# Four block-sum steps instead of three in most gate-and-up pairs of a two-layer encoder, with the matching order of steps and of the work around them

## The chip, the cores and the metric

The kernel runs on one core of one Trainium2 chip. The metric is the device time of one execution in microseconds. The engines go by these names: PE is TensorE (matmuls; PEld its weight loads), DVE is VectorE, ACT is ScalarE, POOL is GpSimd, SP is the engine that issues most loads.

## The reference

Two layers on 256 tokens of 2048 features, all in float32. Layer 0 mixes tokens by attention, layer 1 by a gated recurrence; each layer then has a feed-forward part with 5632 hidden features. Per layer:

```
x = x + mixer(rms_norm(x, g_mix))
x = x + (silu(h @ w_gate) * (h @ w_up)) @ w_down      # h = rms_norm(x, g_ffn)
```

The feed-forward parts hold most of the matmuls. The change touches these and the place where layer 0 hands over to layer 1.

## The kernel before

**Three matmuls for one product.** Every float32 operand is split into a rounded part `hi` (fp32r) and the rest `lo`. A product is hi*hi + hi*lo + lo*hi, three matmuls (`product`, L354 to L359). The tokens are the stationary side (128 x 128 tiles, two token halves), the weights the moving side, 512 columns wide.

**Splitting the weights.** `load_half` (L126) loads a half tile of 128 x 1024 weights over SP's queue into one of five `raw` buffers; ACT rounds it into `hi` (L141), DVE subtracts to get `lo` (L142). Both have five buffers as well.

**Pairs.** `project_pair` (L345) computes two groups of 512 output columns at once. For gate and up these are the same columns of `w_gate` and `w_up`. There are 11 such pairs ("units") in a layer, each with eight steps over the 2048 inputs, a step being two input tiles of 128. The hidden features are worked in three parts of 12, 16 and 16 tiles (`PARTS`): three units, then four, then four. After each part, two down pairs multiply its hidden tiles into the 2048 outputs, with six steps in part 0 and eight in parts 1 and 2. The last down pair of layer 0 is worked one column group at a time.

**Block-sum steps.** A plain step is a 2 x 2 block product (two token halves by two column groups, over two input tiles): eight products, 24 matmuls. Some steps are worked with seven products, 21 matmuls (Strassen's scheme in Winograd's form). These need sums and differences of the weight blocks (`seven_forms`, L308) and of the input blocks (`x_forms`, L333). One of the two weight half tiles is combined by a pair of POOL transfers, a plain one and an accumulating one, into `sr` (two buffers, `fetch_next`, L299). SP loads a quarter into `wx`. DVE adds three blocks (L319, L323, L324), ACT rounds (L321, L322, L326), and DVE splits (L325, L327, L328). `wx`, `wxh` and `wxl` have one buffer each. Four of the seven products of a pair collect in four PSUM banks of their own (`p1`, `q5`, `q6`, `q7` from `ps_m`). After the last block-sum step of a pair, `merge` (L399) combines them into `fg` and `fu`, with one ACT copy and four DVE operations.

**Which steps.** `THREE` gives the block-sum steps of a pair as input step numbers 1, 3 and 5. The first unit of a layer has two (3 and 5), the others three. Down pairs with eight steps have three, part 0's have none, and the last down pair of layer 0 has none. `pair_plan` (L154) works the steps up to the last block-sum step for both column groups together, and the rest one group at a time.

**The end of a unit.** `done` (L839) adds the PSUM sums to the merged ones (L843, L846) and applies SiLU and the gating (L847). Then the hidden tile is turned by a 32 x 32 transposition (L860) into `tb`, by sixteen ACT copies (L866) into `tf`, and by a split (L873, L874). These pieces are put on the list `owed` and emitted during the next pair's steps by `settle`.

**What sets the order.** PE's instructions run in program order. The other engines' order comes from a scheduler, with explicit ties on top: `in_line` keeps the weight splits of ACT and of DVE in order, `follow` ties one instruction behind another, and `not_after` together with `settled` puts an instruction ahead of the DVE split that comes some halves later. `later` puts off a piece by a number of half-steps (`clock`).

**The hand-over between layers.** `Norm.add` prepares the next normalised input from each finished 512 columns: squares (L491), transposition (L496), copies into `tf` (L503), and scaled and split operands (L478, L479). For the last columns `finish` (L518) works out the inverse root mean square first, and `spread` brings it into a row by a small matmul (L536), 20 half-steps later (`NORM`). Then `project_two` and `conv_branch` begin the recurrence.

Of the kernel before, what the change touches and what calls it, by code (L numbers as in the profile page):

```python
# [27 lines left out]
PARTS = [12, 16, 16]  # L28
THREE, TWO, SHORT = (1, 3, 5), (2, 5), 6
READY = 6  # L30
FIRST_STEPS = (0, 1, 2, 4, 3, 6, 5, 7)
# [10 lines left out]
WARM = 10  # L42
NORM = 20
FIRST = 6
# [26 lines left out]
def trunk(ctx, tc, w, out):  # L71
# [45 lines left out]

    def not_after(i, ahead=3):
        due.setdefault(taken[0] + ahead, []).append(i)

    def settled(i, n):
        for k in [k for k in due if k <= n]:
            for j in due.pop(k):
                follow(i, j)

    def load_half(src, n, pieces=1, then=None, before=None):  # L126
        raw = wp.tile([P, HALF, P], F32, tag="raw", name=nm("raw"), bufs=5)
        hi = wp.tile([P, HALF, P], F32R, tag="hi", name=nm("hi"), bufs=5)
        lo = wp.tile([P, HALF, P], F32R, tag="lo", name=nm("lo"), bufs=5)
        for i in range(pieces):  # L130
            sl = slice(i * n // pieces, (i + 1) * n // pieces)
            newest["load"] = sync.dma_start(out=raw[:, sl, :], in_=src[:, sl, :])
        newest["raw"] = raw
        if then:
            then()
        if before:
            before(raw)
        for i in range(pieces):
            sl = slice(i * n // pieces, (i + 1) * n // pieces)
            newest["tiles"] = hi, lo  # L140
            newest["cast"] = in_line("act", act.copy(hi[:, sl, :], raw[:, sl, :]))  # L141
            rest = in_line("dve", dve.tensor_tensor(lo[:, sl, :], raw[:, sl, :], hi[:, sl, :].bitcast(F32), ALU.subtract))  # L142
            settled(rest, taken[0] - 1)
        return [(hi[:, i, :], lo[:, i, :]) for i in range(n)]
# [12 lines left out]
    def unit_seven(i):  # L157
        return THREE[1:] if i == 0 else THREE

    def unit_plan(i):  # L160
        steps = range(KT // 2) if i else FIRST_STEPS
        return pair_plan(steps, 1 + steps.index(unit_seven(i)[-1]))
# [8 lines left out]
    def down_seven(n, alone):  # L171
        return () if alone else () if n == SHORT else THREE

# [171 lines left out]
    def project_pair(xs, forms, plan, middle, done, ready=None):  # L345
# [19 lines left out]
        for i, (n, cols) in enumerate(plan):  # L365
            if n in forms:
                s1, s2, s3, s4 = forms[n]
                b11, b21, t3, b22, t1, t2, t4 = seven_forms()
                settle(3)
                if n == seven[0]:  # L370
                    p1, q6, q5, q7 = (ps_m.tile([P, WIDE], F32, tag="pm", name=nm("pm")) for _ in range(4))
                last = n == seven[-1]
                product(p1, tokens(2 * n, 0), b11, last)
                product(bank(0, 0), tokens(2 * n + 1, 0), b21)
                product(bank(1, 0), s4, b22)
                product(q7, s3, t3, last)
                product(q5, s1, t1, last)
                product(q6, s2, t2, last)
                product(bank(0, 1), tokens(2 * n + 1, 1), t4)
                if last:  # L380
                    middle(p1, q5, q6, q7)
                continue
            if len(cols) == 1 and i and len(plan[i - 1][1]) == 2:
                settle(-1)
                if ready:
                    ready()
            end = n == plan[-1][0]
            for j in cols:
                half()
                if i:  # L390
                    settle(2 if len(owed) > 6 else 1)
                hi, lo = (flat(t) for t in newest["tiles"])
                for a in range(2):
                    for k in range(2):
                        product(bank(j, a), tokens(2 * n + k, a), (hi[:, k, :], lo[:, k, :]), end and k == 1)
                if end:
                    done(j, banks[j])

    def merge(p1, q5, q6, q7):  # L399
# [4 lines left out]
        dve.tensor_tensor(g[:, 1, :], q7, g[:, 1, :], ALU.subtract)  # L404
        dve.tensor_tensor(u[:, 1, :], u[:, 0, :], q7, ALU.subtract)
        return g, u
# [58 lines left out]
    class Norm:  # L465
# [6 lines left out]
        def operand(self, x, wide=False):  # L472
# [5 lines left out]
            i = act.activation(hi, x, AF.Copy, scale=g)  # L478
            dve.scalar_tensor_tensor(lo, x, g, hi.bitcast(F32), ALU.mult, ALU.subtract)  # L479
            self.xs.append(t)  # L480
# [3 lines left out]
        def add(self, c):  # L484
# [4 lines left out]
            def first():  # L489
                for a in range(2):  # L490
                    act.activation(tmp("nj", (P, WIDE), mybir.dt.bfloat16, 1), x_tok[:, a, c, :], AF.Square, accum_out=self.sums[:, a, c : c + 1])  # L491
                fields["behind"] = self.finish() if last else [line.get(e) for e in ("act", "dve")]
                fields["b"] = fp[0].tile([P, 2, FOUR, P], F32, tag="tb", name=nm("tb"))
                fields["f"] = fp[0].tile([P, 8, FOUR, 32], F32, tag="tf", name=nm("tf"))
                for a in range(2):
                    dve.transpose(fields["b"][:, a, :, :], x_tok[:, a, c, :])  # L496

            def copies(q):
                b, f = fields["b"], fields["f"]
                behind = fields["behind"] if last else [line.get(e) for e in ("act", "dve")]  # L500
                for i in range(4):
# [5 lines left out]
            def operands():  # L507
                for k in range(FOUR):
                    self.operand(fields["f"][:, :, k, :], True)
                for n in THREE[1:] if self.seven else ():  # L510
                    if FOUR * c <= 2 * n < FOUR * c + FOUR:
# [6 lines left out]
        def finish(self):  # L518
# [4 lines left out]
            if not self.seven:  # L523
                return prev[0], self.spread()


        def spread(self):
            dg = tmp("ndg", bufs=1)
            for a in range(2):
                i = dve.tensor_scalar(dg[:, a * P : (a + 1) * P], ident, self.rt[:, a : a + 1], None, ALU.mult)  # L530

# [7 lines left out]

            later(NORM, stage)  # L540
            return i

# [288 lines left out]
    def ffn(norm, nxt):  # L831
# [4 lines left out]
        def unit(hid, hid_units, forms, parts, i):  # L836
# [21 lines left out]
            def transposes():  # L858
                kept["b"], kept["f"] = (fp[0].tile([P, 2 * FOUR, P], F32, tag=n, name=nm(n), bufs=1) for n in ("tb", "tf"))
                dve.transpose(kept["b"], got[1])  # L860

            def copies(q):
                b = kept["b"][:].rearrange("p (a i) (k t) -> p a i k t", a=2, k=FOUR)
                f = kept["f"][:].rearrange("p q (k t) -> p q k t", k=FOUR)
                for i in range(4):
# [3 lines left out]
            def split_tiles():  # L869
                f = kept["f"][:].rearrange("p q (k t) -> p k q t", k=FOUR)  # L870
                h = act_tiles()
# [7 lines left out]

            owed.extend([transposes, *(partial(copies, q) for q in range(4)), split_tiles])  # L880

        line.update(act=None, dve=None)
# [118 lines left out]
    for b in range(-1, NBLK):  # L1001
# [9 lines left out]
        if nxt:  # L1011
            accs = (project_sum(nr.xs) for _ in range(2)) if blk else project_two(nr.xs, FOUR)
            nxt.xcs = [conv_branch(2 * b + 2 + i, t) for i, t in enumerate(accs)]
# [108 lines left out]
```

## Time and profile before

| | us |
|---|---|
| median of three runs | 1966.99 (1964.8 to 1967.59) |
| the profiled execution | 1964.75 |
| its span, first to last instruction | 1963.0 |
| layer 0's feed-forward part | 259.7 to 949.9 |
| layer 1's feed-forward part | 1271.2 to 1963.0 |
| granted TensorE clock | 1.00 throughout |

The stages' bounds are read from where the matmuls of each part begin. Rows of the profile give start and length in us, the engine, the line of the kernel, and what is written from what; rows that group instructions give their count, their busy time, the mean length in ns, and the idle time of the engine before them with what ended it. A window of stretches gives each engine's busy time in each.

### The profile page before, as it was taken

How to read it: one execution, taken by the hardware profiler on the slowest of the kernel's cores; microseconds unless marked ns; L12 is line 12 of the kernel's file. 1: busy time of each engine (PE TensorE's matmuls, PEld its weight loads, DVE VectorE, ACT ScalarE, POOL GpSimd, SP SyncE). 2: the span in 40 equal slices, each digit the busy share in tenths (PEclk: the TensorE clock that was granted, in tenths of full speed). 3: DMA queues.
4: the chain of work that ended last, by engine and by line, in shares of the span. 5: the costliest groups of instructions: out<-in, count | busy, mean ns of one | idle time of the engine just before them, and what ended most of it. 6: DMA issues, size and time to landing. Idle time of an engine off the chain costs nothing.

```text
span 1963.0 us, 27585 instructions
## 1 busy us (share of the span) xinstructions
PE 1954.5 (100%) x9665; PEld 1660.3 (85%) x9665; DVE 1686.6 (86%) x2274; ACT 1344.2 (68%) x2051; POOL 222.3 (11%) x317
## 2 busy tenths in 40 slices
PE   9999999999999999999999999999999999999999
PEld 8888888888888888888899998888888888888887
DVE  6776989858999989999788986998768999989997
ACT  6666767655677556777799996767646776567763
POOL 0011000000011100101034331001001010011010
PEclk9999999999999999999999999999999999999999
DMA  8543667756677876776555546567757777677784
GB/s 340 186 140 140 209 207 243 237 202 225 207 247 243 267 247 215 232 233 232 193 176 174 195 160 219 194 205 239 250 189 226 239 239 256 232 242 236 233 261 164
DMA packets 134059, 430.75 MB, mean 219 GB/s; under 512 B 15008, under 2 KB 15904, under 8 KB 133664
## 3 DMA queue, kind: packets, MB, share of 16 engines
q1 hardware_dynamic: 109296, 362.11, 52.9%
q0 software_dynamic: 24480, 66.86, 13.2%
q8 instruction: 76, 1.25, 0.2%
q14 instruction: 63, 0.52, 0.1%
q10 hardware_dynamic: 144, 0.02, 0.0%
HBM read 426.83 MB, written 2.10 MB: 219 GB/s over the span
## 4 chain that ended last, share of the span: by engine, by line
PE 98%; ACT 1%; DVE 1%; issue 0%; DMA 0%; DVEq 0%; ACTq 0%
PE acc L356 63%; PE pm L356 12%; PE acc L272 10%; PE acc L410 3%; PE acc L409 3%; PE acc L411 3%; PE pm L272 1%; PE pm L410 1%; PE pm L409 1%; PE pm L411 1%; PE pm L743 1%; PE pm L775 1%; PE pm L761 0%; ACT sg L607 0%; ACT L607 0%
## 5 line engine op out<-in xcount | busy, mean ns | idle before, releaser
L142 DVE TENSOR_TENSOR lo<-raw,hi 128x1024 fp32r<-128x1024 f32 (+1 forms) x621 | 748.4, 1229 | 130.6 <-ACT hi L141 127.7
L141 ACT CAST hi<-raw 128x1024 fp32r<-128x1024 f32 (+1 forms) x621 | 638.0, 1046 | 310.4 <-PE acc L356 163.3
L356 PE MATMUL acc<-hi,xg 128*128 128x512 f32 x1920 | 612.7, 389 | 0.0
L356 PE MATMUL acc<-hi,act 128*128 128x512 f32 x1370 | 433.7, 390 | 0.2 <-DVE gl L920 0.2
L356 PEld LDWEIGHTS acc<-hi,xg 128*128 128x128 f32 x1920 | 360.4, 188 | 74.8
L356 PE MATMUL acc<-lo,xg 128*128 128x512 f32 x960 | 373.4, 389 | 0.0
L356 PEld LDWEIGHTS acc<-hi,act 128*128 128x128 f32 x1370 | 257.2, 188 | 53.6 <-DVE gl L920 0.7
L356 PE MATMUL acc<-lo,act 128*128 128x512 f32 x685 | 266.6, 389 | 0.0
L356 PEld LDWEIGHTS acc<-lo,xg 128*128 128x128 f32 x960 | 180.2, 188 | 37.4
L326 ACT CAST wxh<-raw 128x1024 fp32r<-128x1024 f32 x85 | 89.3, 1051 | 91.3 <-DVE raw L324 91.3
L356 PEld LDWEIGHTS acc<-lo,act 128*128 128x128 f32 x685 | 128.6, 188 | 26.0
L866 ACT COPY tf<-tb 32x256 f32<-32x256 f32 x352 | 142.1, 404 | 10.9 <-DVE tb L860 7.0
L409 PE MATMUL acc<-xg,hi 128*128 128x256 f32 x512 | 144.9, 283 | 1.1 <-ACT xg L478 1.1
L410 PE MATMUL acc<-xg,hi 128*128 128x256 f32 x512 | 144.8, 283 | 0.1
L411 PE MATMUL acc<-xg,lo 128*128 128x256 f32 x512 | 144.4, 282 | 0.0
L304 POOL DMA_DIRECT2D sr<-in_w_up_dram x64 | 35.6, 557 | 763.5 <-DVE lo L325 598.1
L321 ACT CAST hi<-sr 128x1024 fp32r<-128x1024 f32 x85 | 89.3, 1051 | 37.6 <-PE acc L356 27.1
L322 ACT CAST wxh<-wx 128x512 fp32r<-128x512 f32 x85 | 52.8, 621 | 90.1 <-DVE wx L319 55.0
L328 DVE TENSOR_TENSOR wxl<-raw,wxh 128x1024 fp32r<-128x1024 f32 x85 | 103.3, 1215 | 7.7 <-ACT wxh L326 7.5
L272 PE MATMUL acc<-hi,xg 128*128 128x512 f32 x320 | 107.6, 396 | 0.5 <-ACT hi L141 0.5
L325 DVE TENSOR_TENSOR lo<-sr,hi 128x1024 fp32r<-128x1024 f32 x85 | 103.6, 1218 | 0.0
L409 PEld LDWEIGHTS acc<-xg,hi 128*128 128x128 f32 x512 | 97.9, 191 | 1.3 <-ACT xg L478 1.3
(212 smaller groups left out, 3174.5 us busy)
## 6 DMA issues: line engine op xcount, KB each, us to landing
raw<-in_w_gate_dram SPq DMA_DIRECT2D x176, 512.0 KB, 5.3
raw<-in_w_down_dram SPq DMA_DIRECT2D x155, 512.0 KB, 5.1
raw<-in_w_up_dram SPq DMA_DIRECT2D x112, 512.0 KB, 5.4
sr<-in_w_up_dram POOLq DMA_DIRECT2D x64, 512.0 KB, 4.9
raw<-in_w_in_dram SPq DMA_DIRECT2D x64, 512.0 KB, 4.4
raw<-in_w_qkv_dram SPq DMA_DIRECT2D x46, 512.0 KB, 4.4
raw<-in_w_o_dram SPq DMA_DIRECT2D x32, 512.0 KB, 3.5
wx<-in_w_up_dram SPq DMA_DIRECT2D x64, 256.0 KB, 4.6
```

Of the source, the lines that this page charges most:

```text
L141: newest["cast"] = in_line("act", act.copy(hi[:, sl, :], raw[:, sl, :]))
L142: rest = in_line("dve", dve.tensor_tensor(lo[:, sl, :], raw[:, sl, :], hi[:, sl, :].bitcast(F32), ALU.subtract))
L272: pe.matmul(accs[a], x, wt[:, k, :], start=(k0 + k == 0 and n == 0), stop=(end and k == 1 and n == 2))
L321: in_line("act", act.copy(hi, raw))
L325: settled(in_line("dve", dve.tensor_tensor(lo, raw, hi[:].bitcast(F32), ALU.subtract)), taken[0] - 1)
L326: in_line("act", act.copy(xh[:, 1:, :], r1))
L328: in_line("dve", dve.tensor_tensor(xl[:, 1:, :], r1, xh[:, 1:, :].bitcast(F32), ALU.subtract))
L356: pe.matmul(acc, a, b, start=id(acc) not in begun, stop=last and i == 2)
L409: pe.matmul(o, hi, x[:, :S], start=start, stop=False)
L410: pe.matmul(o, hi, x[:, S:], start=False, stop=False)
L411: pe.matmul(o, lo, x[:, :S], start=False, stop=stop)
L866: n = act.copy(f[32 * i : 32 * i + 32, q::4, :, :], b[32 * q : 32 * q + 32, :, i, :, :])
```

## The change

- `MORE = (3, 5, 1, 6)`: the third and later units of each layer have four block-sum steps. `LATER_STEPS` orders their eight input steps so that these stand at places 1, 3, 5 and 7. The first two units stay as they are. Part 0's down pairs, which had none, get the steps 1 and 3.
- The block differences of the inputs of step 6, needed for that, are made once a layer, after the second unit. Room for them comes from `tf`, which is dropped: turned tiles use the merged tile `fg` again.
- In a pair's first step, if it is a block-sum step, nothing owed is emitted, and the products of `bank(0, 1)` and `bank(1, 0)` come last.
- `merge`'s last operation gets a bound by `not_after`, and the bounds now exist for ACT as well as for DVE.
- At the hand-over the root mean square comes behind the last operands (which get bounds on both engines), and its small matmul 31 half-steps later instead of 20. The last copies are no longer tied behind it. The two column groups that begin the recurrence are both projected before either goes on.

```diff
+MORE = (3, 5, 1, 6)
+LATER_STEPS = (3, 0, 5, 2, 1, 4, 6, 7)
-NORM = 20
+NORM = 31
...
-    def not_after(i, ahead=3):
-        due.setdefault(taken[0] + ahead, []).append(i)
-    def settled(i, n):
-        for k in [k for k in due if k <= n]:
+    def not_after(i, ahead=3, eng="dve"):
+        due.setdefault((taken[0] + ahead, eng), []).append(i)
+    def settled(i, n, eng="dve"):
+        for k in [k for k in due if k[0] <= n and k[1] == eng]:
...
+            settled(newest["cast"], taken[0] - 1, "act")
...
-        return THREE[1:] if i == 0 else THREE
+        return THREE[1:] if i == 0 else THREE if i == 1 else MORE
-        steps = range(KT // 2) if i else FIRST_STEPS
+        steps = FIRST_STEPS if i == 0 else tuple(range(KT // 2)) if i == 1 else LATER_STEPS
...
-        return () if alone else () if n == SHORT else THREE
+        return () if alone else THREE[:2] if n == SHORT else THREE
...
-                settle(3)
+                if i:
+                    settle(3)
...
-                product(bank(0, 0), tokens(2 * n + 1, 0), b21)
-                product(bank(1, 0), s4, b22)
+                first = [(bank(0, 0), tokens(2 * n + 1, 0), b21)]
+                rest = [(bank(0, 1), tokens(2 * n + 1, 1), t4), (bank(1, 0), s4, b22)] if n == plan[0][0] else []
+                for t in first if rest else first + [(bank(1, 0), s4, b22)]:
+                    product(*t)
...
-                product(bank(0, 1), tokens(2 * n + 1, 1), t4)
+                for t in rest or [(bank(0, 1), tokens(2 * n + 1, 1), t4)]:
+                    product(*t)
...
-        dve.tensor_tensor(u[:, 1, :], u[:, 0, :], q7, ALU.subtract)
+        not_after(dve.tensor_tensor(u[:, 1, :], u[:, 0, :], q7, ALU.subtract))
...
-                fields["behind"] = self.finish() if last else [line.get(e) for e in ("act", "dve")]
+                if last and self.seven:
+                    self.finish()
-                fields["f"] = fp[0].tile([P, 8, FOUR, 32], F32, tag="tf", name=nm("tf"))
+                fields["f"] = fp[1].tile([P, 8, FOUR, 32], F32, tag="fg", name=nm("fg"), bufs=1)
...
+                if last and not self.seven:
+                    for e, i in zip(("act", "dve"), newest["operand"]):
+                        not_after(i, 4, e)
+                    self.finish()
...
-                kept["b"], kept["f"] = (fp[0].tile([P, 2 * FOUR, P], F32, tag=n, name=nm(n), bufs=1) for n in ("tb", "tf"))
+                kept["b"] = fp[0].tile([P, 2 * FOUR, P], F32, tag="tb", name=nm("tb"), bufs=1)
+                kept["f"] = got[0][:].rearrange("p a (q t) -> p (a q) t", t=P)
...
+            if i == 1:
+                n = MORE[-1]
+                norm.forms[n] = x_forms(norm.xs[2 * n], norm.xs[2 * n + 1], f"nf{n}")
...
-            accs = (project_sum(nr.xs) for _ in range(2)) if blk else project_two(nr.xs, FOUR)
+            accs = (project_sum(nr.xs) for _ in range(2)) if blk else list(project_two(nr.xs, FOUR))
```

More of the change, by code (lines that the diff above doesn't have):

```diff
@@ L478, in operand @@
             i = act.activation(hi, x, AF.Copy, scale=g)
-            dve.scalar_tensor_tensor(lo, x, g, hi.bitcast(F32), ALU.mult, ALU.subtract)
+            newest["operand"] = i, dve.scalar_tensor_tensor(lo, x, g, hi.bitcast(F32), ALU.mult, ALU.subtract)
             self.xs.append(t)
@@ L499, in copies @@
                 b, f = fields["b"], fields["f"]
-                behind = fields["behind"] if last else [line.get(e) for e in ("act", "dve")]
+                behind = None if last else [line.get(e) for e in ("act", "dve")]
                 for i in range(4):
@@ L523, in finish @@
             if not self.seven:
-                return prev[0], self.spread()
+                self.spread()
         def spread(self):
@@ L529, in spread @@
             for a in range(2):
-                i = dve.tensor_scalar(dg[:, a * P : (a + 1) * P], ident, self.rt[:, a : a + 1], None, ALU.mult)
+                dve.tensor_scalar(dg[:, a * P : (a + 1) * P], ident, self.rt[:, a : a + 1], None, ALU.mult)
             def stage():
@@ L540, in spread @@
             later(NORM, stage)
-            return i
     fp = []
@@ L863, in copies @@
                 b = kept["b"][:].rearrange("p (a i) (k t) -> p a i k t", a=2, k=FOUR)
-                f = kept["f"][:].rearrange("p q (k t) -> p q k t", k=FOUR)
+                f = kept["f"].rearrange("p q (k t) -> p q k t", k=FOUR)
                 for i in range(4):
@@ L869, in split_tiles @@
             def split_tiles():
-                f = kept["f"][:].rearrange("p q (k t) -> p k q t", k=FOUR)
+                f = kept["f"].rearrange("p q (k t) -> p k q t", k=FOUR)
                 h = act_tiles()
```

## The prediction

> **What bounds the kernel now.** I read the page first, then the chain of waits, then TensorE's own waits, then a table of stretches cut at the pairs of column groups, and last the timelines of one dense pair.
>
> ```profile
> span 1963.0 us, 27585 instructions
> PE 1954.5 (100%) x9665; PEld 1660.3 (85%) x9665; DVE 1686.6 (86%) x2274; ACT 1344.2 (68%) x2051; POOL 222.3 (11%) x317
> ...
> PE 98%; ACT 1%; DVE 1%; issue 0%; DMA 0%; DVEq 0%; ACTq 0%
> ```
>
> TensorE is busy throughout and is 98% of the chain. So a matmul taken away is worth its full spacing as long as the operands still come in time. The chain gives the spacing: 27 matmuls in 6.12 us, 0.2267 us each.
>
> ```profile
> 459.62 6.12 PE acc L356 x27
> ```
>
> In all the feed-forward work TensorE waits for nobody. Two of its waits lie where layer 0's feed-forward ends:
>
> ```profile
> PE pm L536 <- DVE ndg L530: 1.6, 1, 1.6
> PE acc L409 <- ACT xg L478: 1.1, 1, 1.1
> ```
>
> Whether operands can come faster is a question of VectorE. The stretches below, in order: the two down pairs of part 0, a middle gate-and-up pair of part 1, and that part's two down pairs.
>
> ```profile
> core 0: us, PE busy (x) PEld busy (x) DVE busy (x) ACT busy (x) POOL busy (x), PEclk, DMA share, GB/s
> 384.82:417.46 32.64, 32.64 (x146) 27.03 (x145) 20.06 (x20) 19.75 (x29) 0.00 (x0) 1.00 0.63 209
> 417.46:450.10 32.64, 32.64 (x146) 27.03 (x145) 18.81 (x19) 13.18 (x13) 0.00 (x0) 1.00 0.52 187
> 533.06:574.54 41.48, 41.48 (x185) 34.35 (x184) 39.65 (x51) 30.01 (x44) 4.24 (x6) 1.00 0.75 243
> 616.02:657.50 41.48, 41.48 (x185) 34.35 (x184) 39.56 (x47) 28.08 (x40) 4.26 (x6) 1.00 0.74 237
> 657.50:698.98 41.48, 41.48 (x185) 34.35 (x184) 38.56 (x46) 22.07 (x24) 4.25 (x6) 1.00 0.76 252
> ```
>
> Part 0's down pairs leave VectorE 40% free; the dense pair leaves it 1.83 us of 41.48. How little is in hand there shows in one operand: VectorE's last split of a block-sum step ends at 549.63 + 1.23 = 550.86, and the matmul that reads its second piece starts at 552.17, a reserve of 1.3 us.
>
> ```profile
> 549.63 1.23 DVE L328 TENSOR_TENSOR wxl<-raw,wxh 128x1024 fp32r<-128x1024 f32 x1 [0.26 <-ACT wxh L326]
> ```
> ```profile
> 552.17 0.39 PE L356 MATMUL pm<-wxl,nf 128*128 128x512 f32 x1
> ```
>
> **How many steps are added.** A block-sum step is 21 matmuls in place of 24.
>
> ```profile
> L319 DVE TENSOR_TENSOR wx<-wx,raw 128x512 f32<-128x512 f32 x85 | 58.2, 685 | 2.1 <-DMA wx<-in_w_down_dram 1.9 <-DMA wx<-in_w_up_dram 0.2
> ```
>
> The 85 are 2 + 10 x 3 in the gate-and-up pairs of each layer and 21 in the down pairs. The change adds one in nine pairs per layer (18) and two in each of part 0's two down pairs per layer (8): 26 steps, 111 in all. TensorE saves 26 x 3 x 0.2267 = 17.7 us.
>
> **What one step costs VectorE.** Spacings of back-to-back instructions count, since durations overlap by about 0.08 us:
>
> ```profile
> 555.92 0.76 DVE L337 TENSOR_TENSOR tb<-act 128x256 f32<-128x256 f32 x2
> ...
> 557.19 0.49 DVE L339 TENSOR_TENSOR tb<-tb 128x128 f32<-128x128 f32 x2
> ...
> 558.20 1.22 DVE L325 TENSOR_TENSOR lo<-sr,hi 128x1024 fp32r<-128x1024 f32 x1
> 559.33 0.68 DVE L327 TENSOR_TENSOR wxl<-wx,wxh 128x512 fp32r<-128x512 f32 x1
> 559.93 0.28 DVE L339 TENSOR_TENSOR tb<-tb 128x128 f32<-128x128 f32 x1
> ...
> 561.47 3.49 DVE L142 TENSOR_TENSOR lo<-raw,hi 128x1024 fp32r<-128x1024 f32 x3
> 564.88 0.69 DVE L402 TENSOR_TENSOR fg<-pm,fg 128x512 f32<-128x512 f32 x1
> ...
> 576.01 1.41 DVE L847 SCALAR_TENSOR_TENSOR fu<-fu,nr,fg 128x512 f32<-128x512 f32 x2
> ...
> 579.67 1.24 DVE L860 STREAM_TRANSPOSE tb<-fu 128x1024 f32<-128x1024 f32 x1
> ```
>
> A split of 1024 columns takes 1.13 us (558.20 to 559.33; three from 561.47 to 564.88 agree), an operation of 512 takes 0.60. A block-sum step is three of the first and four of the second, 5.8 us; a plain step is two splits, 2.27. Each added step costs VectorE 3.5 us and gives TensorE 0.68 less time. In the dense pair, 39.65 + 3.5 = 43.2 us then stand against 40.80: **VectorE becomes the slower engine there**, by 2.1 to 2.4 us a pair, and catches up in the down pairs.
>
> **The ledger.** I follow the reserve at that last split from one block-sum step to the next. With steps at places 1, 3, 5 and 7 TensorE takes 45 x 0.2267 = 10.2 us from one to the next, and VectorE's bare work is 5.8 + 2.27 = 8.1. On top come: from place 7 to the next pair's place 1 the merge (four of 0.60) and four evictions (0.60 each), 12.9 in all, reserve -2.7; from 1 to 3 the gating (1.33) and the transposition (1.16), -0.4; from 3 to 5 the split of the hidden tiles (1.13) and the block differences (two adds 0.68, four subtractions 0.82, one split 0.61), -1.1; from 5 to 7 nothing, +2.1. The reserve has a ceiling: the sums' tile has one buffer, so its casts (below; 0.53 from start to start, and 1.05 less the overlap, 0.97) and the last split (1.13) follow TensorE's leaving the step before, with a hand-over of 0.1 (my estimate); the reader comes 5.44 + 15 x 0.2267 = 8.84 after that, which leaves 6.1. The first pair of a part has neither tiles nor transposition of a pair before it and starts from there.
>
> Second pair: 3.4, 3.0, 1.9, 4.0. Third: 1.3, 0.9, then 0.2 us short, 2.1. Fourth: short by 0.6, 0.4, 1.1, then 2.1. Into the down pair TensorE has 15.6 us and VectorE 17.7: even. So TensorE waits 2.3 us in a part of four pairs; there are four of those, 9.2 us. In part 0 only the third pair is dense; it starts about 0.3 in hand and is short by some 1.2, twice: 2.5. The down pairs of part 0 cost VectorE 2 x 3.5 + 2.4 (merge) + 2.4 (additions) each, 11.8 on top of 19 to 20: about 31.3 against a TensorE time of 31.3. Their block differences, 2 x 2.1, fall into the pairs before, and the extra differences for block step 6 (2.1 a layer, in the second pair) have until place 7 of the third. No wait is booked there; cover gone, all of this is 11 us over both layers.
>
> **Whether VectorE stands idle besides.** In the dense pair it waits only for ScalarE, 1.8 us, because the sixteen copies of the transposed tile run in one piece ahead of the cast that it needs:
>
> ```profile
> DVE wxl L327 <- ACT wxh L322: 1.5, 1, 1.5
> DVE wxl L328 <- ACT wxh L326: 0.3, 1, 0.3
> ```
> ```profile
> 541.37 6.63 ACT L866 COPY tf<-tb 32x256 f32<-32x256 f32 x16
> 548.02 0.62 ACT L322 CAST wxh<-wx 128x512 fp32r<-128x512 f32 x1
> 548.55 1.05 ACT L326 CAST wxh<-raw 128x1024 fp32r<-128x1024 f32 x1
> ```
>
> With the new places twelve of the sixteen are put off until the step at place 3 has been emitted, and each copy is tied behind the newest cast in line, so they come after that step's L326. I take this idle time as 0. The bounds are 0 and 1.8 us in each of 16 dense pairs (three in each of four parts, two in part 0 of each layer), 28 us.
>
> **The rest.** The root mean square now stands behind the last operands, and its matmul comes 31 instead of 20 half-steps on. That removes the 1.1 us wait, if the operands are ready; the 1.6 us one may stay: taken -1.1, bounds 0 and -2.7. POOL's two transfers a step (0.55 and 0.86 us of issue) and SP's one stay off the path while the buffers hold; SP's load of wx waits for L327, and the raw loads behind it wait too:
>
> ```profile
> SPq L316 <- DVE wxl L327: 450.2, 71, 11.2
> ```
>
> Five raw buffers cover that now, at the same distance of 10.2 us between such steps. Reusing `fg` for the transposed tile makes the next merge wait for L874, some three steps earlier: nothing. The first step's new product order costs no matmul. TensorE's order is written by hand, so the added steps do run.
>
> **Sum.** The profiled execution took 1964.75 us (span 1963.0): 1964.75 - 17.7 + 9.2 + 2.5 - 1.1 = 1957.7. The median of the runs, 1966.99, lies 2.2 above that execution, so I say 1960.
>
> **Rivals.** (a) VectorE keeps up everywhere: 1967.0 - 17.7 - 2.7 = 1946.6. For it: 40% free in part 0's down pairs; against it: 43.2 over 40.8. (b) **Slower:** the copies on ScalarE still stand ahead of the casts, at whatever place, or equal holes open as VectorE's fixed order meets a late TensorE. Then nothing absorbs the 1.8 us a dense pair: 1960 + 28 = 1988. It turns the sign from 0.45 us a pair on (7.1 / 16). For it: it is in every dense pair now, and ScalarE gets 1.7 us more a step (four casts of 1.05, 1.05, 0.62 and 1.05 for two of 1.05); against it: the new tie. (c) The prefetched blocks come late:
>
> ```profile
> sr<-in_w_up_dram POOLq DMA_DIRECT2D x64, 512.0 KB, 4.9
> ...
> sr<-in_w_up_dram POOLq DMA_DIRECT2D x64, 256.0 KB, 7.1
> ```
> ```profile
> 538.28 0.55 POOL L304 DMA_DIRECT2D sr<-in_w_up_dram  x1 [13.87 <-ACT wxh L326]
> 542.65 0.86 POOL L305 DMA_DIRECT2D sr<-in_w_up_dram  x1 [3.81 <-DMA sr<-in_w_up_dram]
> ```
> ```profile
> 553.29 1.06 ACT L321 CAST hi<-sr 128x1024 fp32r<-128x1024 f32 x1
> ```
>
> A buffer is refilled from 538.28 to 542.65 + 7.1 = 549.8 and read at 553.3, two steps on: 3.5 us to spare. Each us beyond that costs one per two of the 72 steps in the nine pairs, so 1 us over gives 1960 + 36 = 1996. [...]
>
> **Chances.** Forecast 0.40 (own range 1953 to 1967), (a) 0.17, (b) 0.33, (c) 0.04, mixtures 0.06. This kernel's runs tell 0.2%, 3.9 us, from nothing. Faster: 0.32 + 0.17 + 0.01 = 0.50; same: 0.08 + 0.05 + 0.01 = 0.14; slower 0.36. The range, 1947 to 1982, leaves out a part of (a) below, and above it the full (b) and (c).
>
> **What would show it.** Right: TensorE waits for L325, L327 or L328 late in the third and fourth pair of a part, about 12 us in all, none in the first; DVE above 97% there; the idle time before L327 near 0. Wrong: waits in first pairs, waits for PSUM evictions or for `sr`, or idle time of VectorE beside TensorE's.

## The result and the profile after

| | us |
|---|---|
| median of four runs | 2069.58 (2066.73 to 2070.28) |
| the kernel before, same comparison | 1966.07 |
| ratio | 1.0524, interval 1.0511 to 1.0537 |
| the profiled execution | 2066.73, span 2065.0 |

The change makes the kernel 5.2% slower. Forecast was 1960, with a range to 1982. Two lines of the changed kernel's page, then TensorE's waits (us in total, times, longest):

```profile
PE 1989.3 (96%) x9587; PEld 1663.5 (81%) x9587; DVE 1803.3 (87%) x2478; ACT 1386.5 (67%) x2113; POOL 259.6 (13%) x369
...
PE 67%; DVE 17%; ACT 8%; issue 6%; DMA 1%; POOL 0%; DVEq 0%; ACTq 0%; POOLq 0%; SPq 0%
```
```profile
PE acc L359 <- ACT hi L143: 45.7, 14, 3.4
PE acc L359 <- DVE lo L145: 8.1, 14, 0.8
PE pm L359 <- DVE lo L328: 4.3, 2, 2.2
PE pm L416 <- issue: 4.1, 1, 4.1
```

78 matmuls are gone, as 26 steps should give. Yet the chain, 98% TensorE before, now runs through VectorE and ScalarE for a quarter of its length. The new waits are 14 of 2.5 to 3.4 us: once in each of seven pairs of each layer, namely all four-step pairs that have a tile of the pair before to turn. (The lines have moved by a few: the splits L142, L325, L327, L328 of before are L145, L328, L330, L331 here, the casts L141 and L326 are L143 and L329, the copies L866 are L878, the transposition L860 is L872.)

The table of stretches (columns as in the prediction), one dense pair from merge to merge, and a stretch inside another:

```profile
538.80:587.30 48.50, 43.97 (x183) 35.06 (x182) 43.10 (x56) 31.77 (x47) 5.66 (x8) 0.96 0.69 216
517.47:524.30 6.83, 4.96 (x11) 3.59 (x12) 5.45 (x6) 5.74 (x7) 0.00 (x0) 0.50 0.65 167
```

The dense pair takes 48.5 us, against 41.48 before. VectorE, the fourth figure, is busy for 43.10 of it, very near the 43.2 of the forecast. So VectorE is not what fills the pair: it stands idle for 5.4 us. Where, is shown by the timelines of VectorE, then ScalarE, then TensorE around the step at place 3 of the pair just ahead of it, which has the same two holes (start, length, and the idle time before with what ended it):

```profile
512.80 1.22 DVE L331 TENSOR_TENSOR wxl<-raw,wxh 128x1024 fp32r<-128x1024 f32 x1 [0.54 <-ACT wxh L329]
518.85 3.50 DVE L145 TENSOR_TENSOR lo<-raw,hi 128x1024 fp32r<-128x1024 f32 x3 [4.83 <-ACT hi L143]
```
```profile
510.05 1.65 ACT L878 COPY fg<-tb 32x256 f32<-32x256 f32 x4 [2.44 <-DVE tb L872]
511.72 1.05 ACT L329 CAST wxh<-raw 128x1024 fp32r<-128x1024 f32 x1
512.80 4.96 ACT L878 COPY fg<-tb 32x256 f32<-32x256 f32 x12
517.78 2.94 ACT L143 CAST hi<-raw 128x1024 fp32r<-128x1024 f32 x3
```
```profile
515.12 0.39 PE L359 MATMUL acc<-wxh,xg 128*128 128x512 f32 x1
518.88 0.80 PE L359 MATMUL acc<-hi,xg 128*128 128x512 f32 x1 [3.37 <-ACT hi L143]
520.13 0.79 PE L359 MATMUL acc<-lo,xg 128*128 128x512 f32 x1 [0.46 <-DVE lo L145]
```

ScalarE does four copies, the cast L329, then the other twelve copies in one piece, and only then the casts of the weights of place 4. VectorE finishes L331 at 514.02 and has nothing it may do until the first of these casts is done: 4.83 us. With the 0.54 before L331 that is the 5.4. TensorE arrives at place 4 as well and waits 3.37.

The stages, from where the matmuls of each begin:

| span in us | up to the recurrence | recurrence | w_out and layer 1's feed-forward | all |
|---|---|---|---|---|
| before | 949.7 | 233.8 | 779.5 | 1963.0 |
| after | 998.2 | 238.1 | 828.7 | 2065.0 |

Each layer's feed-forward loses some 49 us, and the recurrence 4.3.

### The profile page after: what moved, and what is told of

Its sections match the earlier page's. It is cut to its first block, busy times and chain, and to the rows that moved or that the text cites. A ratio compares the mean times of both kernels' runs of the same rounds, so it can differ in the third digit from the quotient of the medians.

```text
span 2065.0 us, 27854 instructions
## 1 busy us (share of the span) xinstructions
PE 1989.3 (96%) x9587; PEld 1663.5 (81%) x9587; DVE 1803.3 (87%) x2478; ACT 1386.5 (67%) x2113; POOL 259.6 (13%) x369
## 4 chain that ended last, share of the span: by engine, by line
PE 67%; DVE 17%; ACT 8%; issue 6%; DMA 1%; POOL 0%; DVEq 0%; ACTq 0%; POOLq 0%; SPq 0%
PE acc L359 38%; PE acc L275 10%; PE pm L359 8%; DVE lo L145 6%; ACT fg L878 4%; PE acc L416 2%; PE acc L417 2%; PE acc L418 2%; ACT wxh L329 1%; DVE lo L328 1%; DVE raw L326 1%; ACT hi L143 1%; PE pm L275 1%; DVE wx L322 1%; DVE wxl L331 1%
## 5 line engine op out<-in xcount | busy, mean ns | idle before, releaser
L145 DVE TENSOR_TENSOR lo<-raw,hi 128x1024 fp32r<-128x1024 f32 (+1 forms) x595 | 711.4, 1226 | 138.9 <-ACT hi L143 131.4
L143 ACT CAST hi<-raw 128x1024 fp32r<-128x1024 f32 (+1 forms) x595 | 601.8, 1044 | 174.2 <-PE acc L359 50.5
L359 PE MATMUL acc<-hi,xg 128*128 128x512 f32 x1668 | 562.0, 403 | 45.7 <-ACT hi L143 45.7
L359 PEld LDWEIGHTS acc<-hi,xg 128*128 128x128 f32 x1668 | 326.5, 196 | 120.7 <-ACT hi L143 51.8
L359 PE MATMUL acc<-lo,xg 128*128 128x512 f32 x834 | 338.0, 405 | 8.1 <-DVE lo L145 8.1
L325 ACT CAST wxh<-wx 128x512 fp32r<-128x512 f32 x111 | 69.0, 622 | 230.3 <-DVE wx L322 192.9
L329 ACT CAST wxh<-raw 128x1024 fp32r<-128x1024 f32 x111 | 116.7, 1052 | 112.1 <-DVE raw L327 111.6
L878 ACT COPY fg<-tb 32x256 f32<-32x256 f32 x352 | 142.0, 403 | 36.6 <-DVE tb L872 32.6
L416 PE MATMUL acc<-xg,hi 128*128 128x256 f32 x512 | 145.2, 284 | 0.0
L331 DVE TENSOR_TENSOR wxl<-raw,wxh 128x1024 fp32r<-128x1024 f32 x111 | 134.9, 1215 | 10.1 <-ACT wxh L329 10.1
L328 DVE TENSOR_TENSOR lo<-sr,hi 128x1024 fp32r<-128x1024 f32 x111 | 135.0, 1216 | 0.0
L307 POOL DMA_DIRECT2D sr<-in_w_up_dram x82 | 45.5, 556 | 646.8 <-DVE lo L328 390.9
L308 POOL DMA_DIRECT2D sr<-in_w_up_dram x82 | 70.8, 863 | 361.6 <-DMA sr<-in_w_up_dram 333.2
L359 PE MATMUL pm<-wxh,nf 128*128 128x512 f32 x328 | 115.3, 392 | 0.0
```

Of the source, the lines that this page charges most:

```text
L328: settled(in_line("dve", dve.tensor_tensor(lo, raw, hi[:].bitcast(F32), ALU.subtract)), taken[0] - 1)
L329: in_line("act", act.copy(xh[:, 1:, :], r1))
L331: in_line("dve", dve.tensor_tensor(xl[:, 1:, :], r1, xh[:, 1:, :].bitcast(F32), ALU.subtract))
L359: pe.matmul(acc, a, b, start=id(acc) not in begun, stop=last and i == 2)
L416: pe.matmul(o, hi, x[:, :S], start=start, stop=False)
L878: n = act.copy(f[32 * i : 32 * i + 32, q::4, :, :], b[32 * q : 32 * q + 32, :, i, :, :])
```

## The experiments

Theory A: the loss lies in the four-step pairs, where ScalarE's copies stand ahead of the casts for place 4 while VectorE has no reserve left. Rivals: VectorE's load alone; TensorE's half clock (0.50 in the stretch above) around the new waits; the hand-over. Unless said otherwise, each run is the changed kernel with one edit.

**Three steps again, the rest of the change kept.**

```diff
-        return THREE[1:] if i == 0 else THREE if i == 1 else MORE
+        return THREE[1:] if i == 0 else THREE
...
-        steps = FIRST_STEPS if i == 0 else tuple(range(KT // 2)) if i == 1 else LATER_STEPS
+        steps = FIRST_STEPS if i == 0 else tuple(range(KT // 2))
...
-            if i == 1:
+            if False:
```

> Gate-and-up pairs as before (three block-sum steps), the rest changed: two steps in the down pairs of part 0, the hand-over. Theory A (only the new places make the block of copies harmful): no wait of 3 us in the pairs; eight steps save 5.4 us, the hand-over costs about 5.7, so 1963 to 1970 us. Theory B (VectorE's load decides): part 0's down pairs, with 31.3 us of VectorE work against 31.3, wait 2 us or more each, 1972 us or more.

Measured 1967.64 us, ratio 1.0010 (1.0000 to 1.0020). TensorE's first two waits:

```profile
PE pm L416 <- ACT hi L143: 3.9, 1, 3.9
PE acc L359 <- DVE act L886: 2.2, 2, 1.1
```

No wait of that kind is left in a gate-and-up pair, as theory A expected. All but 2 of the 103 us go with the four-step pairs and the block differences of step 6 that are made for them (the last line of the edit); the wait at L416 stays.

**The copies spread.** One group of four copies for each thing emitted in the block-sum steps.

```diff
-                    settle(3)
+                    settle(1)
```

> Theory A (the twelve copies in one piece ahead of the next casts on ScalarE make each dense pair wait, and the wait brings the halved clock): the 14 waits of 3.4 us for L143, the 0.5 us behind each and about 41 us of the clock's loss go, so 1965 to 1980 us, clock 0.997 or more. Theory B (VectorE is short of time in a dense pair, 43.2 us against 40.8, and would wait at another place): the waits move to the splits L328 and L331 and the time stays above 2030 us.

Measured 2080.58 us, ratio 1.0588 (1.0572 to 1.0604): slower still. VectorE's timeline, a dense pair's stretch and TensorE's longest wait:

```profile
516.41 1.23 DVE L331 TENSOR_TENSOR wxl<-raw,wxh 128x1024 fp32r<-128x1024 f32 x1 [0.54 <-ACT wxh L329]
519.17 1.23 DVE L145 TENSOR_TENSOR lo<-raw,hi 128x1024 fp32r<-128x1024 f32 x1 [1.53 <-ACT hi L143]
521.91 1.23 DVE L145 TENSOR_TENSOR lo<-raw,hi 128x1024 fp32r<-128x1024 f32 x1 [1.51 <-ACT hi L143]
524.65 1.22 DVE L145 TENSOR_TENSOR lo<-raw,hi 128x1024 fp32r<-128x1024 f32 x1 [1.52 <-ACT hi L143]
```
```profile
542.50:591.10 48.60, 44.04 (x183) 34.66 (x182) 43.39 (x56) 31.89 (x47) 5.66 (x8) 0.96 0.71 216
```
```profile
PE acc L359 <- DVE lo L328: 49.4, 24, 3.3
```

One hole of 4.83 us became three of 1.5: four copies now stand ahead of each cast. Theory A missed. The signs of theory B came, TensorE's waits moved to L328 and the time stayed above 2030, but its reason didn't: VectorE is still idle for 5.2 us of the pair. It isn't the length of a single piece that counts, but that copies and casts alternate on ScalarE while VectorE consumes each cast as soon as it is there. Why the run is 11 us slower than the changed kernel was not traced.

**TensorE kept busy.** Fifteen matmuls with a tile of zeros are added ahead of place 4 in four-step pairs. They add nothing to the sums and fill the gap.

```diff
+            if i == 3 and plan[0][0] in forms:
+                for _ in range(15):
+                    pe.matmul(bank(0, 0)[: 3 * P // 4, :], zero, xs[0], start=False, stop=False)
...
+    zero = cst.tile([P, 3 * P // 4], F32R, tag="zero", name="zero")
...
+    dve.tensor_tensor(zero, ones[:, : 3 * P // 4], ones[:, : 3 * P // 4], ALU.subtract)
```

> Fifteen matmuls by a tile of zeros are added at place 4 of each dense pair, where TensorE waits; they add nothing to the sums. Theory A1 (the slow matmuls after each wait come from the idle time of TensorE itself): the granted clock stays at 1.00 in these pairs and the time falls by about 40 us to 2027, while VectorE still waits 4.8 us for L143. Rival A2 (they are slow for another reason, a late operand or contention): the clock and the slow matmuls stay, and the time is 2067 us or more.

Measured 2075.91 us, ratio 1.0562 (1.0541 to 1.0583). The dense pair, and the stretch around its place 4:

```profile
540.90:589.40 48.50, 46.49 (x197) 35.60 (x196) 43.08 (x56) 31.66 (x47) 5.68 (x8) 1.00 0.72 218
517.00:524.00 7.00, 6.24 (x27) 4.23 (x26) 3.07 (x3) 6.91 (x12) 0.86 (x1) 1.00 0.69 177
```

The granted clock is 1.00 in both, and the pair is 48.50 us long as it was. So the half clock cost nothing in these pairs: time that a faster TensorE gains there it then spends waiting for VectorE (its waits for VectorE's splits came to 26.4 us in all, against 16.6 in the changed kernel). The fifteen matmuls also stand in the four pairs 3 and 7 (counted from 0), where there was no gap, and add 15 x 0.2267 = 3.4 us to each. Without these 13.6 us the run would be at 2062 by my estimate, 7 below the changed kernel, not the about 40 that theory A1 expected.

**Fewer copies.** Of the tiles of the third and later pairs, twelve of the sixteen copies are left out, so part of the hidden values is old data. VectorE's instructions stay the same.

```diff
-            def copies(q):
+            def copies(q, skip=i >= 2):
+                if skip and q:
+                    return
```

> Of the sixteen ScalarE copies of a turned hidden tile only the first four are made in the third and later pairs of a layer; the other twelve are left out, so the hidden tiles are not the right ones. Theory A (VectorE's idle time of 5.4 us in each of 14 dense pairs, put there by the copies on ScalarE, is the loss; with it gone the ledger of the prediction holds): the idle time goes, a dense pair takes 41 to 43 us instead of 48.4, and the time is 1960 to 1980 us. Theory B (VectorE's own 43 us of work is the loss and the copies only decide where it waits): the pairs stay at 46 us or more and the time above 2030 us.

Measured 2004.16 us, ratio 1.0198 (1.0177 to 1.0218), between both expectations.

```profile
531.80:575.36 43.56, 42.32 (x182) 33.28 (x181) 42.98 (x56) 26.69 (x35) 5.66 (x8) 1.00 0.78 243
```

The dense pair falls by 4.9 us, the size of the hole, and VectorE is now busy 42.98 of 43.56. That is the other part: VectorE alone holds the pair 2.8 us above TensorE's 40.8.

**VectorE lighter as well.** For the same tiles all copies (the last four on ScalarE too) and the transposition are left out, and the block differences of those hidden tiles are replaced by those of the input. By the rows below this takes 2.4 to 3.1 us of VectorE's work out of a dense pair.

```diff
-                dve.transpose(kept["b"], got[1])
+                if i < 2:
+                    dve.transpose(kept["b"], got[1])
...
-            def copies(q):
+            def copies(q, skip=i >= 2):
+                if skip:
+                    return
...
-                        forms[n] = x_forms(hid[2 * n], hid[2 * n + 1], f"hf{k}")
+                        forms[n] = x_forms(hid[2 * n], hid[2 * n + 1], f"hf{k}") if i < 2 else norm.forms[n]
```

> The run with 12 of 16 copies left out took 2004 us, its dense pairs 43.55 us with VectorE busy 42.98. Here, beside that, all copies and the transposition of the hidden value are left out from the third pair on and the block differences of the hidden value are replaced by those of the input, which lightens VectorE by about 3 us in a dense pair. Theory A (with the hole gone VectorE's own load sets the pair): the dense pair falls to TensorE's 40 to 41.5 us and the time to 1955 to 1975. Rival (the four-step places themselves hold TensorE up, by another wait): the pair stays above 43 us, the time above 1995.

Measured 1982.21 us, ratio 1.0083 (1.0064 to 1.0102). Two dense pairs, and what TensorE still waits for:

```profile
530.90:572.16 41.26, 40.17 (x178) 32.92 (x177) 40.63 (x49) 24.88 (x30) 5.66 (x8) 1.00 0.83 258
572.16:613.51 41.35, 41.21 (x182) 33.81 (x181) 39.86 (x47) 24.99 (x29) 5.66 (x8) 1.00 0.82 251
```
```profile
PE acc L359 <- DVE lo L328: 5.7, 8, 1.3
PE pm L359 <- DVE lo L328: 4.3, 2, 2.1
PE acc L359 <- ACT hi L143: 3.3, 2, 2.9
```

The pair itself does what theory A said (40 to 41.5), the whole time doesn't (1955 to 1975). The waits of 2.1 and 2.9 us that stay lie in the third pair. The 2.9 are ScalarE's: that pair's turned tile comes from the second and kept its copies. The 2.1 come at its first step, ahead of those copies. The recurrence keeps its 4 us too.

**Copies where ScalarE waits anyway.** All sixteen are done, but in four-step pairs the groups are emitted just ahead of the cast L325 at places 3, 5 and 7, where ScalarE waits for the sum of the blocks.

```diff
-    def seven_forms():
+    def seven_forms(n=0):
...
         in_line("act", act.copy(hi, raw))
+        settle(n)
         in_line("act", act.copy(xh[:, 0, :], x))
...
-                b11, b21, t3, b22, t1, t2, t4 = seven_forms()
-                if i:
+                dense = n == plan[0][0] or begun_dense
+                begun_dense = dense
+                b11, b21, t3, b22, t1, t2, t4 = seven_forms((0, 0, 1, 1, 2, 2, 2, 2)[i] if dense else 0)
+                if i and not dense:
                     settle(3)
...
-                if i:
+                if i and (not begun_dense or i == 1 and j == 0):
                     settle(2 if len(owed) > 6 else 1)
```

> The sixteen copies are kept and put ahead of the casts L325 of the steps at places 3, 5 and 7, where ScalarE waits for VectorE's sums anyway (2.3 to 2.7 us each). Theory A: as with the twelve copies left out, within 10 us of it: 1965 to 1985 us. Theory B or a lack of ScalarE time (the copies delay L325 and L329 instead): the idle time moves before L330 and L331 and the time stays above 2030 us.

Measured 2018.15 us, ratio 1.0269 (1.0252 to 1.0286).

```profile
531.60:576.48 44.88, 42.41 (x178) 33.60 (x177) 43.38 (x56) 31.52 (x46) 5.68 (x8) 0.96 0.77 234
```

51 us come back with every copy done, so the hole is a matter of order. What is left is mostly VectorE, 43.38 of 44.88, and the time lies between the two expectations. The same with the old hand-over:

> As the run with the copies ahead of L325, and the hand-over of the kernel before. Theory A: the recurrence stage is 4.4 us shorter, and the time is lower by that if TensorE bounds what follows: 1961 to 1981 us. Rival (VectorE bounds layer 1 and takes the gain back, as in the first run with the old hand-over): no change against that run.

It took 2015.06 us, ratio 1.0253 (1.0238 to 1.0268), 3 us less. The recurrence itself isn't shorter, 238.6 us against 238.4, so theory A missed.

**Four steps in two pairs a layer only.** Pairs 3 and 7, the first of their parts, have no tile to turn; here only they have four steps, with part 0's steps and the old hand-over (whose lines are left out below).

```diff
-        return THREE[1:] if i == 0 else THREE if i == 1 else MORE
+        return THREE[1:] if i == 0 else MORE if i in (3, 7) else THREE
...
-        steps = FIRST_STEPS if i == 0 else tuple(range(KT // 2)) if i == 1 else LATER_STEPS
+        steps = FIRST_STEPS if i == 0 else LATER_STEPS if i in (3, 7) else tuple(range(KT // 2))
```

> Four steps only in the pairs 3 and 7 of each layer, which follow a down pair and have no tile to turn, three in the others; two in part 0's down pairs; the hand-over as in the kernel before. Theory A (only pairs that also turn a tile run out of VectorE and ScalarE time): no wait above 2 us; 12 steps save 8.2 us, part 0 waits 2.2: 1959 to 1962 us. Rival (four steps at places 1, 3, 5, 7 cost by themselves): waits in the pairs 3 and 7 or behind them, 1970 us or more.

Measured 1975.02 us, ratio 1.0048 (1.0033 to 1.0063). The run with three steps everywhere took 1967.64, so this one costs 7 us more where TensorE's work falls by 2.7. But the loss doesn't lie in the four-step pairs. The stretches below are cut at merges. The first two, with three steps everywhere and here, go from the second pair's merge to that of part 0's last down pair; the next two, in the same order, go from there to the same place in part 1 and hold pair 3:

```profile
331.97:434.74 102.77, 101.68 (x448) 83.55 (x447) 98.61 (x120) 70.21 (x99) 9.94 (x14) 1.00 0.77 240
332.21:437.51 105.30, 103.28 (x448) 82.97 (x447) 100.68 (x127) 70.79 (x99) 9.95 (x14) 1.00 0.75 234
434.74:683.62 248.88, 248.88 (x1100) 206.15 (x1099) 232.56 (x281) 163.33 (x219) 25.56 (x36) 1.00 0.77 244
437.51:686.16 248.65, 248.65 (x1097) 205.27 (x1096) 235.23 (x286) 164.08 (x221) 26.99 (x38) 1.00 0.78 244
```

In layer 1 the first stretch grows from 102.75 to 107.00 us. The two together are 6.8 us longer, and the spans of the two runs differ by 6.2. The one edit that falls into this stretch is the block differences of step 6, which are made there for the later pairs: VectorE, the fourth figure, is busy for 2.1 us more. Part 1, where pair 3 has a fourth step and nothing to turn, is 0.2 us shorter, of the 0.7 that three matmuls are worth. Theory A missed the time, its rival the place.

**Part 0's steps alone.** The kernel before, with two block-sum steps in part 0's down pairs.

```diff
-        return () if alone else () if n == SHORT else THREE
+        return () if alone else THREE[:2] if n == SHORT else THREE
```

> The kernel before with only part 0's two down pairs of each layer given block sums at steps 1 and 3 (8 steps added, 24 matmuls of 0.227 us fewer, about 5.4 us of TensorE). There VectorE has no value to transpose, no copies of ScalarE stand ahead of the casts. Theory A (a four-step pair loses because a turned tile's 16 copies stand ahead of the casts; where no tile is turned the steps pay): 1960 to 1963 us. Rival (any added step costs VectorE or a wait more than it saves): 1966 to 1972.

Measured 1961.56 us, ratio 0.9978 (0.9969 to 0.9987). The two down pairs of part 0:

```profile
384.10:416.05 31.95, 31.69 (x140) 25.86 (x140) 30.11 (x38) 23.00 (x35) 2.84 (x4) 1.00 0.74 234
416.05:448.00 31.95, 31.95 (x143) 26.46 (x142) 31.31 (x38) 16.10 (x18) 2.83 (x4) 1.00 0.71 239
```

VectorE goes from 20 to 30 us and still stays below TensorE, so the steps pay, as theory A expected. It is the fastest kernel of this study, 0.2% below the one before. With the two steps at 1 and 2 instead:

> As the run before, with the two steps at 1 and 2 in place of 1 and 3, so that the second step's sums are asked for before the gating product that frees the next operand. If a wait of about a microsecond at step 4 of part 0 is what steps at 1 and 3 leave, this takes 2 us off: 1959 to 1961. Rival: the second sums are now the late ones and it is the same or 1 us slower than the run before.

it took 1969.3 us, ratio 1.0020 (1.0010 to 1.0029), 7.7 us more than at 1 and 3; both expectations missed. TensorE's longest waits there:

```profile
PE acc L356 <- ACT hi L141: 2.2, 2, 1.2
PE acc L356 <- DVE act L874: 1.9, 2, 1.0
```

Two block-sum steps in a row ask for 11.6 us of VectorE within two steps of TensorE, 42 x 0.2267 = 9.5 us; the distance between the steps is worth more than the wait that I meant to avoid.

**The hand-over.** First the changed kernel with the old hand-over:

> The hand-over between the layers as in the kernel before (root mean square ahead of the operands, 20 half-steps, one column group after the other), the rest changed. Theory A: the hand-over's own part is a loss: the wait of 4.1 us before L416 and the 1.0 us behind it go, with a halved clock of 6.8 us (3.4 us lost), and the old 2.8 us come back, so about 5.7 us less, 2061 us. Rival: the wait there is a result of the late pairs before it and comes back in another form: 2065 us or more.

2069.55 us, ratio 1.0530 (1.0509 to 1.0551), no change, as the rival had it: the recurrence is shorter by 2.7 us, and layer 1 gives it back. Then the kernel before with the new hand-over (order, `NORM`, bounds, `list(project_two(...))`), its turned tile still in `tf`:

> The kernel before with the new hand-over alone (the recurrence's operands made ahead, the step that follows behind them). The changed kernel's recurrence is 4.4 us longer than before. Theory A (the hand-over itself costs this: the 2.8 us of old waits go, and a wait of about 4 us at the first matmul of the recurrence with a half-clock stretch after it comes): 1969 to 1972 us. Rival (those 4.4 us came from the pairs running late behind it): 1964 to 1967.

1965.73 us, ratio 1.0000 (0.9991 to 1.0010), its recurrence 234.2: theory A missed, the reordered hand-over costs nothing. The changed kernel's hand-over differs from this one in the buffer of its turned tile. Five views show it: SP's loads of the gate weights (L935 before, L950 after) in the timelines of SP, before and after; then, after, VectorE's instruction that ends just ahead of them, ScalarE's cast that needs them, and the row of SP's own waits:

```profile
904.23 0.80 SPq L935 DMA_DIRECT2D graw<-in_w_gates_dram  x2
```
```profile
1006.62 0.80 SPq L950 DMA_DIRECT2D graw<-in_w_gates_dram  x2
```
```profile
1004.86 1.68 DVE L486 SCALAR_TENSOR_TENSOR xg<-fg,pk,xg 128x256 fp32r<-128x256 f32 x4 [1.35 <-ACT xg L485]
```
```profile
1018.52 0.62 ACT L951 CAST ghi<-graw 128x512 fp32r<-128x512 f32 x1 [3.72 <-DMA graw<-in_w_gates_dram]
```
```profile
SPq L950 <- DVE xg L486: 5.7, 1, 5.7
```

Before, the gate weights are asked for at 904.23, 45 us ahead of the recurrence. After, only at 1006.62, when the last reader of `fg` has ended at 1006.54, 8 us into the recurrence. ScalarE then stands 3.72 us at the cast of these weights, with the casts for the projections queued behind. One line decides it, in the run with three steps:

```diff
-                fields["f"] = fp[1].tile([P, 8, FOUR, 32], F32, tag="fg", name=nm("fg"), bufs=1)
+                fields["f"] = fp[0].tile([P, 8, FOUR, 32], F32, tag="tf", name=nm("tf"))
```

> The run with three steps in every pair and the rest of the change took 1967.6 us, its recurrence 238.4 us against 233.7 before; the hand-over alone, its tile in tf, had 234.2. Here that run once more with one line back: the hand-over's turned tile lies in tf again and not in fg, whose last reader in that run is L486 at 957.2 us, just ahead of SP's first loads of the gate weights at 957.4. Theory A (the loads wait for fg, so ScalarE's casts of them stand in the recurrence's first microseconds and hold its other casts): gate loads go out near 904 us, recurrence 233.5 to 234.5, time 1962 to 1964. Rival (it is the reordered hand-over or part 0's steps): gate loads still near 957, recurrence 237 to 239, time 1967 to 1969.

```profile
903.40 0.80 SPq L950 DMA_DIRECT2D graw<-in_w_gates_dram  x2
```

1963.34 us, ratio 0.9989 (0.9980 to 0.9998), the recurrence 234.3: as theory A expected. With four steps this can't be had as it is: the block differences of input step 6 take up the room of `tf`.

## Why the prediction was wrong, point by point

- **Steps and matmuls** held: 78 matmuls fewer, and the row of L322 (L319 before) counts the 111 steps forecast.

```profile
L322 DVE TENSOR_TENSOR wx<-wx,raw 128x512 f32<-128x512 f32 x111 | 75.8, 683 | 13.8 <-DMA wx<-in_w_up_dram 8.9 <-DMA wx<-in_w_down_dram 4.8
```

- **VectorE's work** held: 43.1 us in a dense pair against 43.2, and with it the sentence that VectorE becomes the slower engine there.
- **"I take this idle time as 0"** is the step that failed, and its bounds of 0 to 1.8 us failed with it: 5.4 us a dense pair. The tie behind the newest cast kept the copies from going ahead of that cast; I read it as if they would then be out of the way. It says nothing of the casts that follow, and ScalarE takes the copies before those. The bound of 1.8 us came from a pair in which VectorE still had a reserve to work off while the copies ran. A hole is only as short as the reserve that covers it, and the ledger itself had that reserve at zero in the later pairs. Leaving out twelve of the sixteen copies gave back 63 us of span (2065.0 to 2002.0), moving all of them 48.
- **The ledger** failed as well. It let VectorE's reserve of 6.1 us in a part's first pair, and the down pairs, carry most of the 2.3 us that it loses in each dense pair, and came to 11.7 us in all. With the hole gone the three dense pairs of a part still take 42.7, 43.6 and 43.5 us from merge to merge (the last two are a row above and its neighbour), so no reserve carries them to TensorE's 40.8: some 30 us over the twelve of parts 1 and 2. When VectorE's own work is lightened (with the last four copies gone as well), 21.5 us of span go. Which buffer keeps VectorE from working ahead in the first pairs was not tried.
- **"No wait is booked there"** failed for the extra block differences of step 6. They were to have time until place 7 of the third pair; in the run with four steps in pairs 3 and 7, the stretch of part 0 shown there is 2.5 and 4.3 us longer with them.
- **The hand-over at -1.1** failed in sign: +4.3. The reordering is worth nothing (1.0000); the 4 us come from the reuse of `fg`, of which the forecast looked at the next merge alone. The loads of the gate weights weren't on its list.
- **Part 0's down pairs** were right in kind: VectorE 30 to 31 us, about even with TensorE, and no wait above 0.3 us when they are the only change. Alone they give 0.22%, 3.9 us between the medians, where the forecast had 8 x 0.68 = 5.4. Together with the rest of the change TensorE waits 1.1 us a layer there for the split of the hidden tiles (L886); why was not traced.
- **The rivals.** (a), VectorE keeps up everywhere, fell by the same row that confirms its load. (b), the copies still stand ahead of the casts "at whatever place", is the mechanism seen; its price of 1.8 us a pair was a third of the 5.4 seen in 14 pairs, since it took over the hole of the kernel before. It had a chance of 0.33, and even its 1988 lay outside the range. (c), late prefetched blocks, isn't what holds the changed kernel: ScalarE, whose cast reads them first, waits for these transfers 1.4 us in all. The accumulating transfers landed in 6.2 us in the changed kernel, against 7.1 before, and in 6.4 us in the run with fewer copies, where VectorE is busy 42.98 of a dense pair's 43.56 us (columns: count, size, us from issue to landing):

```profile
sr<-in_w_up_dram POOLq DMA_DIRECT2D x82, 256.0 KB, 6.2
```
```profile
sr<-in_w_up_dram POOLq DMA_DIRECT2D x82, 256.0 KB, 6.4
```

  So these transfers landed no later with VectorE busier (87% of the span after, 86% before). Late loads do appear in the lighter run: ScalarE waits there 8.1 us, in 13 pieces, for the blocks, and VectorE for the quarter that SP loads into `wx`:

```profile
DVE wx L322 <- DMA wx<-in_w_up_dram: 23.9, 23, 2.1
```

- **What would show it.** Waits for splits late in the third and fourth pair were named as right, idle time of VectorE beside TensorE's as wrong. The latter is what the trace has, from the first dense pair of each part on.

How the 102 us of span add up, from one run to the next: 63.0 for the hole (2065.0 to 2002.0 with twelve copies left out), 21.5 for VectorE's load (to 1980.5), 14.4 for what else the fourth step brings (to 1966.1 with three steps); 3.8 for the gate loads (to 1962.3). The last lies 0.7 below the kernel before. The shares hold for this order of the edits. The 14.4 lie in part 0: from the second pair's merge to that of the last down pair the lighter run takes 110.58 and 110.08 us in the two layers, against 102.77 and 102.75 with three steps. From there to the same place in part 1 it takes 248.12 against 248.88. So even with the copies and some of VectorE's work gone, four pairs with a fourth step, 2.7 us of matmuls, bring 0.8 there.

## What to carry to other kernels

Where an engine has no reserve left, the idle time that a table shows before a change is no bound on the idle time after it: list the instructions that stand in the other engine's order between what it has just produced and what is wanted next, and add up their lengths. An order tie says what an instruction follows, not what it stands in front of. And when a buffer is reused, ask not only who writes it next, but which later loads are given its memory and wait for its last reader.

## What the hardware showed that was not expected

- Around 13 of the 14 waits of about 3 us TensorE's granted clock was 0.50 for a while, in pieces of 3.41 or 6.83 us. Seven of the pieces began within the wait (517.47 to 524.30 above, within the wait that ends at 518.88 and 2.35 us after the last matmul began at 515.12), six up to 1.95 us behind its end. The 14th wait, 2.49 us up to 1429.54, had none: the clock was 1.00 from 1426.60 to 1436.40. Two more pieces lie at other waits, one of 6.83 us at the 4.1 us of L416 and one of 3.41 us at one of the two waits of 2.15 us for L328; the other of the two had none. How long the clock is halved doesn't tell what it costs: with zero matmuls in the gap the mean clock rose from 0.979 to 0.997, and the dense pair above stayed at 48.50 us, since VectorE, with its waits for ScalarE's casts (4.8 us the longest), set its pace.
- A wait that is put down to "issue" (4.1 us at L416) was, in the run with three steps, put down to ScalarE's cast; the cause lay two engines back, in SP's queue.
